# A matrix shift in HBM: the 16 DMA engines' rows spaced 8 apart instead of 4

## The chip, the core and the metric

The kernel runs on one core of a Trainium2 chip. The core has compute engines, which have nothing to do here, and 16 DMA engines, which move data between addresses. SyncE (SP in the profile) issues the transfers; its queue of them is called SPq. One issue is split over the DMA engines, and each contiguous run of it is a packet.

The metric is the time of one execution on the device, in microseconds (us). The kernel before took 813.25 us, the median of three runs from 812.37 to 813.68.

## What is computed

```python
def setup_inputs():
    return {
        "x": np.random.randn(8192, 8192).astype(np.float32),
    }

def reference(x: np.ndarray) -> np.ndarray:
    return np.fft.ifftshift(x)
```

The input is 8192 x 8192 in float32, 268 MB; a row has 32 KB. `ifftshift` of an even size moves everything by half the size in both dimensions, with wrapping: the output's row r is the input's row (r + 4096) mod 8192, and within it the two halves of the columns change places. It is a pure move: 268 MB are read and 268 MB are written.

## The kernel before

There is no on-chip stage: every transfer goes from the input in HBM straight to the output in HBM. The helper `copy` (lines 25 to 29) issues one transfer. Its `dims` are a list of [step, count] pairs, slowest first, in elements; the same list is used on both sides, and only the start differs: on the output's side the row and column given, on the input's side these shifted by half the matrix.

A row is cut into four quarters of 2,048 elements (`piece`), 8 KB each. The outer loop goes over the matrix in blocks of 64 rows (`rows`, 16 engines times `apart` = 4). Within a block four transfers are issued, one for each quarter of the columns, in the order first, third, second, fourth of the output (starts 0, `hc`, `piece`, `hc + piece`, where `hc` is 4,096). Each has 64 rows of 8 KB: 512 KB. In all there are 128 x 4 = 512 issues, all on SP's queue, in program order.

The slowest dimension has 64 entries, and each of the 16 DMA engines gets four neighbouring rows of them, so one engine's rows start 4 rows, 128 KB, after those of the engine before it. Over the four transfers of a block each engine moves its four rows whole. The next block starts 64 rows, 2 MB, further on.

Order and waits are put in by the framework: eight semaphores are used in turn, and SP waits before an issue until an earlier transfer with its semaphore has landed. The profile calls `copy`'s issue line 26.

Of the kernel before, what the change touches and what calls it, by code (L numbers as in the profile page):

```python
# [1 line left out]

# [4 lines left out]


ENGINES = 16  # L10


@with_exitstack
def kernel(
    ctx: ExitStack,
    tc: tile.TileContext,
    x: bass.AP,
    out: bass.AP,
):
    nc = tc.nc  # L20
    R, C = x.shape
    hr = R // 2
    hc = C // 2

    def copy(queue, row, col, dims):
        queue.dma_start(
            out=bass.AP(out.tensor, out.offset + row * C + col, dims),
            in_=bass.AP(x.tensor, x.offset + (row + hr) % R * C + (col + hc) % C, dims),
        )


    apart = 4
    piece = hc // 2
    rows = ENGINES * apart
    for row in range(0, R, rows):
        for col in (0, hc, piece, hc + piece):
            copy(nc.sync, row, col, [[C, rows], [1, piece]])


# [1 line left out]
_INS = ['x']  # L41
_OUTS = [((8192, 8192), 'float32')]


def kernel(**inputs):
    import numpy as _np
    import concourse.bacc as _bacc
    import concourse.tile as _tile
    from concourse import mybir as _mybir
    from concourse.bass_utils import run_bass_kernel_spmd as _run  # L50

    nc = _bacc.Bacc("TRN2", target_bir_lowering=False, num_devices=1)  # L52
    arrays, args = {}, []
    for name in _INS:
        a = _np.ascontiguousarray(inputs[name])
        if a.dtype.kind in "iu":
            a = a.astype(_np.int64)
        arrays[f"in_{name}_dram"] = a
        args.append(nc.dram_tensor(f"in_{name}_dram", a.shape, _mybir.dt.from_np(a.dtype), kind="ExternalInput").ap())
    for i, (shape, dtype) in enumerate(_OUTS):  # L60
        dt = _mybir.dt.from_np(_np.dtype(dtype))
        args.append(nc.dram_tensor(f"out_{i}_dram", shape, dt, kind="ExternalOutput").ap())
    with _tile.TileContext(nc) as tc:
        kernel(tc, *args)
    r = _run(nc, [arrays], core_ids=[0])
    got = tuple(r.results[0][f"out_{i}_dram"] for i in range(len(_OUTS)))
    return got[0]
```

## Time and profile before

| | |
|---|---|
| time, median of 3 runs | 813.25 us |
| lowest to highest | 812.37 to 813.68 us |
| the profiled execution, its own time | 811.93 us |
| its span, first to last instruction | 810.2 us |
| TensorE and the other compute engines | no work; POOL 0.2 us for four constants |
| issues | 512 of 512 KB |
| first issue, last issue | 0.7 us, 797.2 us |

The profile describes one execution. Its page divides the span into 40 equal slices and shows for each the busy share of the DMA engines in tenths and the bytes moved per second, counted once a packet (a copy reads and writes them). Another row gives the packets of each DMA queue and the time they took, as a share of the span of 16 engines. The view of the waits of SP's queue tells how long it stood still and for what. Below the views, the trace has a record of each DMA packet (start, duration, size), without the number of its engine, and one of each increment of a semaphore by a transfer that lands: sixteen for an issue, one an engine.

### The profile page before, as it was taken

Reading aid. Unit: us, or ns where it says so; the run is one execution under the profiler, and the core shown is the slowest. Engines: PE = TensorE matmul, PEld = TensorE weight load, DVE = VectorE, ACT = ScalarE, POOL = GpSimd, SP = SyncE. Lnnn points to the kernel's source line nnn. Section 1 sums busy time; section 2 is a strip of 40 time slices with the busy share of each in tenths; the row PEclk is TensorE's granted clock in tenths of the full one; section 3 lists DMA queues with packets and bytes.
Section 4 is the critical chain, followed back from the end, with each engine's and each line's share of the span. In section 5 each row is a group of like instructions: output and inputs, shape, how many; then the busy total and the mean of one; then the engine's idle time right before and its main releaser. Section 6 shows DMA issues by size and latency. Waiting matters only on the chain. (4 is left out here: it accounts for less than half of the span.)

```text
span 810.2 us, 557 instructions
## 1 busy us (share of the span) xinstructions
POOL 0.2 (0%) x4
## 2 busy tenths in 40 slices
POOL 0000000000000000000000000000000000000000
DMA  8999999999999999999999999999999999999998
GB/s 301 334 328 339 330 335 336 334 329 335 337 336 331 331 335 335 329 335 331 339 333 329 339 336 331 339 330 331 337 336 326 337 330 335 333 328 335 326 328 299
DMA packets 40964, 268.50 MB, mean 331 GB/s; under 512 B 8192, under 2 KB 8192, under 8 KB 8192
## 3 DMA queue, kind: packets, MB, share of 16 engines
q1 hardware_dynamic: 40960, 268.47, 99.1%
q14 instruction: 4, 0.03, 0.0%
HBM read 268.44 MB, written 268.44 MB: 663 GB/s over the span
## 5 line engine op out<-in xcount | busy, mean ns | idle before, releaser
L52 POOL MEMSET const-bfloat16-1.0<- 128x1 bf16 x1 | 0.1, 102 | 0.0
L52 POOL MEMSET const-uint8-127<- 128x1 uint8 x1 | 0.1, 102 | 0.0
L52 POOL MEMSET const-float32-0.0<- 128x1 f32 x1 | 0.1, 99 | 0.2 <-issue 0.2
L52 POOL MEMSET const-float32-1.0<- 128x1 f32 x1 | 0.1, 99 | 0.0
## 6 DMA issues: line engine op xcount, KB each, us to landing
out_dram<-in_x_dram SPq DMA_DIRECT2D x512, 512.0 KB, 12.6
```

Source lines behind the costliest of these rows:

```text
L52: nc = _bacc.Bacc("TRN2", target_bir_lowering=False, num_devices=1)
```

## The change

The 16 engines' groups of rows are 8 rows (256 KB) apart instead of 4, and a block has 128 rows instead of 64. One transfer still gives each engine four neighbouring rows of one quarter of the columns. So a block now takes eight transfers: rows 0 to 3 of each engine's eight in the four quarters, then rows 4 to 7 in the four quarters. The pattern has three dimensions: 16 groups, 4 rows, 2,048 elements.

```diff
-    apart = 4
+    apart = 8
+    part = 4
     piece = hc // 2
-    rows = ENGINES * apart
-    for row in range(0, R, rows):
-        for col in (0, hc, piece, hc + piece):
-            copy(nc.sync, row, col, [[C, rows], [1, piece]])
+    for block in range(0, R, ENGINES * apart):
+        for row in range(block, block + apart, part):
+            for col in (0, hc, piece, hc + piece):
+                copy(nc.sync, row, col, [[apart * C, ENGINES], [C, part], [1, piece]])
```

The number of issues (64 x 2 x 4 = 512), their size, their queue and the size of a packet are as before. The order of the instructions on every engine is the same; only the addresses and the shape of the patterns differ.

## The prediction

> **What bounds the kernel now.** I read the page first: span, the forty slices and the queue rows. Then come the windows view over chosen stretches, the waits of the issuing engine, and the view of all instructions that write the output. Behind these I counted the trace's records of single packets and of landings.
>
> ```profile
> span 810.2 us, 557 instructions
> ...
> DMA  8999999999999999999999999999999999999998
> GB/s 301 334 328 339 330 335 336 334 329 335 337 336 331 331 335 335 329 335 331 339 333 329 339 336 331 339 330 331 337 336 326 337 330 335 333 328 335 326 328 299
> DMA packets 40964, 268.50 MB, mean 331 GB/s; under 512 B 8192, under 2 KB 8192, under 8 KB 8192
> ...
> q1 hardware_dynamic: 40960, 268.47, 99.1%
> ...
> HBM read 268.44 MB, written 268.44 MB: 663 GB/s over the span
> ```
>
> The 16 DMA engines are taken for 99.1% of the span, from the second slice to the last but one, at 326 to 339 GB/s. No compute engine does anything. So the time is the engines' packet time, and the question is what a packet's time is made of. By count the 40,960 packets are 32,768 of 8 KB and 8,192 small ones (16 a transfer, 512 transfers): 2,048 and 512 an engine. The windows view (length, POOL, granted clock, DMA share, GB/s) shows that packets can go faster than they mostly do:
>
> ```profile
> 3.00:5.30 2.30, 0.00 (x0) 1.00 0.94 399
> 5.30:8.00 2.70, 0.00 (x0) 1.00 1.02 370
> 8.00:20.00 12.00, 0.00 (x0) 1.00 0.99 328
> ...
> 100.00:200.00 100.00, 0.00 (x0) 1.00 1.00 334
> ...
> 700.00:797.00 97.00, 0.00 (x0) 1.00 1.00 331
> ```
>
> In the first stretch 399 GB/s; a few us later the rate falls to about 330 and stays there. The packet records say why: of the 114 data packets that start between 2.9 and 5.2 us all took 309 ns. Over the whole span 58% still took 307 to 309 ns, the mean is 390 and one in a hundred takes over 840. A small packet took 9 ns. I read 309 ns as what an engine needs for 8 KB when the memory doesn't hold it up, and the rest as stalls in the memory. For one engine:
>
> - unstalled: 2,048 x 309 ns = 632.8 us, 512 x 9 ns = 4.6 us
> - stalls: 2,048 x (389.9 - 309) ns = 165.6 us
> - sum 803.0 us, which is the 99.1% above. The other 7 us of the 810.2 are 2.1 us before the first packet and 5 of gaps and unequal ends.
>
> **Is the issuing side near a limit?** No:
>
> ```profile
> SPq L26 <- DMA out_dram<-in_x_dram: 525.9, 502, 2.0
> ```
> ```profile
> L26 SPq DMA_DIRECT2D out_dram<-in_x_dram x512: 511/511/695, 0.7 to 797.2; - x171
> ...
> DMA to landing us min/median/max: 4.0/12.6/13.2
> ```
>
> SP's queue needs 511 ns for one issue (512 x 0.511 = 262 us) and stands 526 us waiting for transfers to land. A transfer ends every 810.2 / 512 = 1.58 us and lands 12.6 us after its issue, so some eight (12.6 / 1.58) are always queued.
>
> **The change, part by part.** *Unchanged.* 512 issues of 512 KB, four packets of 8 KB to an engine and issue, the same order of the four quarters, the same bytes: 637.4 us of unstalled time, 0 us of change. Small packets too: 0.
>
> *The issue itself.* Its pattern has three dimensions instead of two (16x4x2048 for 64x2048). The trace shows no such issue. Below: 0, since a cheaper issue gains nothing where SP waits for landings anyway. Above: the longest issue seen, 695 ns, so 184 ns x 512 = 94 us more of SP's queue, all of it inside the 526 us of waiting. I take 0. The cover ends at 1.58 us an issue, three times the usual. No new wait is added, and nothing else stands on that queue before the end.
>
> *The jump between blocks.* Now one issue in four starts a new block, 2 MB on; after it, one in eight steps on by some 4 MB, and one in eight by only 128 KB. What a jump costs is seen in the landing records: the mean time of the 16 landings of an issue moves on by 1.541 us for the second quarter, 1.571 for the third, 1.657 for the fourth and 1.527 for the first of the next block; the mean is 1.573. The step that holds the jump is the cheapest of the four, so a jump as such costs nothing. Bounds: 128 jumps x 46 ns (1.573 - 1.527) = 6 us either way. I take 0.
>
> *The distance between the engines.* This is the part that can move the time, and it moves the 165.6 us of stalls alone. Before, one issue's 64 rows are one run of 2 MB, an engine each 128 KB; after, they lie in 16 clusters of four, an engine each 256 KB, over 4 MB. It matters only if the engines are at the same issue at the same time, and they are: the 16 landings of an issue come within 1.76 us (median; 1.4 to 2.2 for nine issues in ten), about one issue's time. So what the memory sees at once is the 16 engines' rows of one issue or of two neighbours, once for reads and once for writes half the matrix away.
>
> That addresses alone make stalls the trace shows: the four quarters differ only in columns, and they take 1.527 to 1.657 us. With the engines 256 KB apart, their addresses at one moment share one more low bit than with 128 KB, and engines e and e+8 lie 2 MB apart instead of 1 MB. If the memory tells its parts apart by such bits, fewer parts serve the same 16 streams. No row of this trace shows another distance, so I bound it by the quarters. At worst every issue goes like the slowest quarter: 512 x (1.657 - 1.573) = 43 us more. At best every issue goes like the fastest: 512 x (1.573 - 1.527) = 23.6 us less. I take it that one more of the four quarters comes to cost what the slowest does: 128 x 0.084 = 10.8 us. I choose so little because the pattern inside an engine, four rows 32 KB apart in four quarters, stays, and because a part that held up two engines in lockstep would push them out of step, up to the eight queued issues.
>
> On the Trainium skill: DMA: Bandwidth & Descriptors, section Latency and other measured facts, gives copies between HBM tensors whose row pitch is a large power of two, and has them slower the larger it is (207 GB/s at 512 KiB, 164 at 2 MiB, 103 at 4 MiB, 214 when padded). It speaks against this change; if the doubled distance cost what its 512 KiB row lost, the median would be an estimated 813.25 x 214 / 207 = 841. The trace runs at 331 GB/s each way with the engines 128 KB apart, above that page's best, so its figures don't carry over; no run here shows another pitch yet.
>
> **Sum.** 803.0 + 0 + 0 + 0 + 10.8 = 813.8 of packet time, and 7 around it: span 821.0. The profiled execution lay 1.7 us above its span (811.9), and the median shown 1.3 above that, so 813.25 + 10.8 = 824.
>
> **Rivals.** *Wider is better (faster).* With the clusters spread over 4 MB, fewer of the 16 streams meet in the same part of the memory, and the stalls shrink. For it: the stalls are a fifth of the time, 42% of packets have one, and 399 GB/s was once reached. Against it: the distances only grow by one power of two, while the four rows of a cluster, which meet most closely, stay. Its price: half of what separates the mean from the fastest quarter, 512 x 23 ns = 11.8 us, gives 801.5; with all of it, 789.7. It decides as soon as the mean issue takes less than 1.573 us.
>
> *Nothing to tell.* Where data lies in the memory depends on so many address bits that the distance doesn't matter: 813. For it: the stalls look random, each slice within 2% of the mean (326 to 339 of 333 inside). Against: the stalls must stay within 1% (1.66 us) for the time to stay within 0.2%, and the quarters differ by 8%.
>
> *Lockstep bites fully (much slower).* All quarters like the slowest: 856. For it, the narrow landing spread; against, that engines can slip.
>
> *The change doesn't do what it says.* If the three-dimensional pattern is cut up in another way, say on fewer than 16 engines or with an issue over 1.58 us, SP becomes the bound: at 1.62 us an issue 512 x 1.62 = 829 us and 7 around it, 836. Nothing in the trace speaks for it; the outer size, 16, is the number of engines.
>
> **How the numbers follow.** A measurement of this kernel can tell about 0.2%, 1.6 us, from no change: its three runs lie between 812.4 and 813.7. Chances: forecast 0.42 (816 to 840), lockstep in full 0.10, issue bound 0.02: slower 0.54. Wider is better 0.34: faster. Nothing to tell 0.12. The range goes from 795, near the lower bound of 789.7, to 852, near the upper of 856; I leave out 0.07 on each side. The likeliest case's own range is 816 to 840.
>
> **What would show it.** Unstalled packets should stay at 309 ns, and 58% of them or fewer should be so; mean packet some 395 ns instead of 390; GB/s in the middle slices near 329 instead of 333; q1's share still about 99%; issues still 511 ns, with SP's wait for landings longer by the same 11 us; time to landing 12.8 us instead of 12.6. If the issue time is up and the wait gone, the steps on SP are wrong. If the mean packet is under 388 ns, the distance acts the other way, and if it moves while the landings spread far wider than 1.8 us, it is the loss of step and not the addresses of one issue. A q1 share well below 99% would mean idle engines, which no step here has.

## The result

The changed kernel is slower by 0.3%: 815.94 us, the median of ten runs (813.33 to 817.51), against 813.16 us for the kernel before in ten runs (811.43 to 813.68). The ratio is 1.0028, its 95% interval 1.0016 to 1.0041. On another chip, where the kernel before took 824.71 us, it was 1.0034 (1.0020 to 1.0049). So the change costs 2 to 3 us. All further kernels are compared with the kernel before on the same chip, by ratios; there it took 823 to 825 us. A run more than 1.5% above the fastest of its kernel is left out of a ratio, which happened only to two of the four runs with 32 rows apart (1129.7 and 1139.75 us; the other two took 1111.89 and 1114.91).

The page of the changed kernel, the rows that answer to those of before:

```profile
span 815.4 us, 557 instructions
...
DMA  8999999999999999999999999999999999999998
GB/s 301 331 331 331 332 329 331 331 329 328 335 333 333 330 333 327 331 333 331 333 330 325 336 329 333 326 334 334 334 325 332 331 334 330 331 331 334 327 332 295
...
q1 hardware_dynamic: 40960, 268.47, 99.7%
...
HBM read 268.44 MB, written 268.44 MB: 658 GB/s over the span
```

Nothing has changed in kind: the DMA engines are taken from end to end, and the rate is lower by a small amount that is spread over all slices (329 GB/s over the span instead of 331). No slice stands out, so no single place of the program lost the time. The profiled executions exaggerate: this one took 817.17 us, one of the slower of its ten, that of before 811.93, one of the faster; their 5.2 us are twice the difference of the medians.

The windows view (length, POOL, clock, DMA share, GB/s) has the same fast start and the same fall:

```profile
3.00:5.30 2.30, 0.00 (x0) 1.00 1.00 406
5.30:8.00 2.70, 0.00 (x0) 1.00 0.96 364
8.00:20.00 12.00, 0.00 (x0) 1.00 1.01 330
...
100.00:200.00 100.00, 0.00 (x0) 1.00 1.00 330
...
805.00:808.00 3.00, 0.00 (x0) 1.00 1.03 333
```

A share over 1 in a stretch this short says little, since the view counts a packet whole where it starts. The packet records say more. The sum of all packets' time grew by 10.3 us an engine (803.0 to 813.3), the span by only 5.2. Up to 20 packets are under way at once, more than there are engines, so some overlap; but this overlap is nearly the same in both kernels (7.3 and 7.6 us an engine). What shrank is the time in which fewer than 16 are under way: 11.1 us an engine before, 6.3 after. So about half of the added packet time filled gaps and cost nothing.

SP's queue, by the waits and by the view of the output's instructions:

```profile
SPq L26 <- DMA out_dram<-in_x_dram: 500.3, 502, 1.6
```
```profile
L26 SPq DMA_DIRECT2D out_dram<-in_x_dram x512: 571/571/705, 0.7 to 802.2; - x171
...
DMA to landing us min/median/max: 4.1/12.6/13.2
```

An issue with the three-dimensional pattern takes 571 ns, 60 ns more than before. Over 512 issues that is 31 us, and the wait for landings shrank by 26 us. The time went into cover, as far as these rows tell.

By the packet records an unstalled packet still takes 309 ns. More of them are unstalled (61% at 307 to 309 ns instead of 58%), yet the mean is 394.9 ns instead of 389.9: the stalls are fewer and longer (a stalled packet takes 530 ns on average instead of 500).

### The profile page after: what moved, and what is told of

Same layout as the page of the kernel before. It is cut to its first block, busy times and chain, and to the rows that moved or that the text cites. A ratio compares the mean times of both kernels' runs of the same rounds, so it can differ in the third digit from the quotient of the medians.

```text
span 815.4 us, 557 instructions
## 1 busy us (share of the span) xinstructions
POOL 0.2 (0%) x4
## 2 busy tenths in 40 slices
DMA packets 40964, 268.50 MB, mean 329 GB/s; under 512 B 8192, under 2 KB 8192, under 8 KB 8192
## 6 DMA issues: line engine op xcount, KB each, us to landing
out_dram<-in_x_dram SPq DMA_DIRECT2D x512, 512.0 KB, 12.6
```

## The experiments

In the diffs `rows`, `part` and `piece` are as in the code above.

**Is it the pattern's shape, or the issue's 60 ns?** The first kernel keeps the rows and engines of before and takes each engine's rows from the last to the first, so that the pattern has three dimensions.

```diff
 # rev4
-            copy(nc.sync, row, col, [[C, rows], [1, piece]])
+            copy(nc.sync, row + apart - 1, col, [[apart * C, ENGINES], [-C, apart], [1, piece]])
```

> The rows and engines of the kernel before (engines 4 rows apart), but each engine takes its four rows from the last to the first, so that the pattern has three dimensions as in the changed kernel. Theory A (the distance between the engines makes the stalls): issue time about 571 ns as in the changed kernel, yet 813 us, since the distance is the old one. Theory B (the three-dimensional issue costs the 2.8 us): 816. Theory C (the order in which an engine comes back to its own rows, halves of a block and jumps): 813, with the jumps of the kernel before.

Measured: 825.3 against 823.15 us, ratio 1.0027 (1.0014 to 1.0040), issue 571 ns. That is what theory B expected, so the shape comes under suspicion. The next runs are the changed kernel again, two kernels that split it by sides, and one that deals the old rows out one by one:

> The changed kernel once more, beside the kernel before on this chip. If its 0.28% holds from chip to chip, the ratio is 1.002 to 1.004. Theory A (the distance between the engines makes the stalls, convexly: 1.0028 at 8, 1.053 at 16) and theory B (the three-dimensional pattern costs it, as the kernel with descending rows had 1.0027 at the old distance) both expect that.

```diff
 # read8_write4 (read4_write8 is the mirror): k = 0, 1 for the two halves of a block of 128 rows
 # copy(queue, output row, input row, column, output's pattern, input's pattern)
+    four = [[4 * C, ENGINES], [C, part], [1, piece]]
+    eight = [[8 * C, ENGINES], [C, part], [1, piece]]
...
+                copy(nc.sync, block + 64 * k, block + 4 * k, col, four, eight)
```

> Reads with the engines 8 rows apart as in the changed kernel, writes 4 apart as before; the rows within each 128 of the output come out in another order. Theory A: if the stalls come from the reads, 1.003; if from the writes, 1.000. Theory B: 1.003 whichever side. If the two single-sided kernels add up to the whole (one 1.003 and one 1.000, or about 1.0015 each), the distance does it; if both have the whole 1.003, it is the pattern's shape.

> The mirror of the kernel above: reads 4 rows apart as before, writes 8 apart as in the changed kernel; rows within 128 come out in another order. Theory A: 1.003 if the stalls come from the writes, 1.000 if from the reads. Theory B: 1.003.

The output of these two isn't the reference's, as their rows come out in another order; they serve for the time alone.

```diff
 # d1
-            copy(nc.sync, row, col, [[C, rows], [1, piece]])
+            copy(nc.sync, row, col, [[C, ENGINES], [ENGINES * C, part], [1, piece]])
```

> The same 64 rows an issue as before, dealt out one by one: engine e takes rows e, e+16, e+32, e+48, so the engines are one row (32 KB) apart and an engine's own rows 512 KB. The pattern has three dimensions. Theory A in the form of distance between engines: not above 1.000. Theory A in the form of which rows are moved at the same time: 1.000, since they are the same 64. Theory B: 1.003.

Measured: the changed kernel 1.0034 (1.0020 to 1.0049), reads at 8 alone 1.0054 (1.0033 to 1.0074), writes at 8 alone 1.0031 (1.0017 to 1.0044), engines one row apart 1.0006 (0.9991 to 1.0021). The last has the three-dimensional pattern and its 571 ns an issue, and no price that can be measured: the shape alone doesn't cost 0.3%. Each side alone costs about as much as both, or more. Theory B had expected 1.003 of each, so these two speak for the shape, though 1.0054 is more than it expected, and against sides that add up; d1 speaks against the shape. A cleaner comparison on the shape comes below.

**Is it the distance, and if so, how?**

```diff
 # d16, d32, d64: the changed kernel with d = 16, 32 or 64
-    apart = 8
+    apart = d
 # d12, d24 in outline: n = 12 or 24; what is left of each half of the rows with 4 rows apart
+    for half in (0, hr):
+        for block in range(half, half + hr, ENGINES * n):
...
+                    copy(nc.sync, row, col, [[n * C, ENGINES], [C, part], [1, piece]])
```

> The changed kernel with the engines 16 rows (512 KB) apart and four passes over a block. Theory A: more than the changed kernel, 819 or above, because the distance doubles once more. Theory B: 816, the same issue. Theory C: 816 or a little more, as three quarters of the steps to new rows are short ones instead of half.

> Engines 12 rows (384 KB) apart, not a power of two; 504 of the 512 issues so, the last 64 rows of each half with 4 rows apart. Theory A in the form of shared low address bits: 813 or less, since 384 KB leaves the low bit of the distance at 128 KB, as in the kernel before. Theory A in the form of sheer distance: between the changed kernel and 16 apart, 817 to 819. Theory B: 816. Theory C: 816 to 817.

> Engines 24 rows (768 KB) apart, farther than the 16 that cost 5.3%, but not a power of two; 480 of 512 issues so, the rest 4 apart. Theory A1 (sheer distance, or the width of memory that is open at once): above 16 apart, 1.06 or more. Theory A2 (a power of two in the distance: the engines meet in the same part of the memory): near 12 apart, 1.01 to 1.02, since three of the 16 engines' low bits differ as 24 = 16 + 8.

> Engines 64 rows (2 MB) apart, 16 passes over a block of 1,024 rows. Theories A1 and A2: clearly above 16 apart, 1.08 or more. If the cost at 16 is a matter of one particular bit of the address and nothing of the distance, it stays at 1.05 or falls.

> Engines 32 rows (1 MB) apart, the missing point between 16 (1.053) and 64 (1.332). If each doubling takes away half of the places that the engines can be in at once, it lies between, near 1.15; the step from 8 to 16 then is where the price begins to be paid.

Measured, all with clusters of four neighbouring rows:

| engines apart | ratio | 95% interval |
|---|---|---|
| 8 rows (the change) | 1.0028, 1.0034 | 1.0016 to 1.0049 |
| 12 | 1.0115 | 1.0095 to 1.0134 |
| 16 | 1.0531 | 1.0515 to 1.0547 |
| 24 | 1.0034 | 1.0020 to 1.0047 |
| 32 | 1.3512 | 1.3474 to 1.3551 |
| 64 | 1.3324 | 1.3272 to 1.3376 |

Sheer distance falls: 24 apart costs next to nothing beside 16. So does "each doubling takes its share", which expected 1.15 at 32 and more at 64: from 8 to 16 the price is multiplied by about 17, from 16 to 32 by 7, and then it stops. 24 costs the same as 8 (1.0034 on both), and both distances are a multiple of 8 rows but not of 16, which fits the form with shared low bits of the address. 12 doesn't fit it: by that form it is like 4, yet it costs more than 24; that isn't explained here. Rows of the pages of the kernels with 16, with 24 and with 32 rows apart:

```profile
GB/s 282 311 313 312 307 317 312 312 314 315 310 314 309 315 314 316 313 311 316 308 310 316 313 308 313 311 313 314 305 312 311 316 306 313 314 312 319 308 306 274
...
q1 hardware_dynamic: 40960, 268.47, 99.4%
...
out_dram<-in_x_dram SPq DMA_DIRECT2D x512, 512.0 KB, 13.4
```
```profile
HBM read 268.44 MB, written 268.44 MB: 651 GB/s over the span
...
out_dram<-in_x_dram SPq DMA_DIRECT2D x512, 512.0 KB, 12.8
```
```profile
q1 hardware_dynamic: 40960, 268.47, 99.0%
...
HBM read 268.44 MB, written 268.44 MB: 484 GB/s over the span
...
out_dram<-in_x_dram SPq DMA_DIRECT2D x512, 512.0 KB, 17.2
```

The share of the DMA engines is 99% in the fast and in the slow ones: it can't tell a good layout from a bad one. The rate and the time to landing (12.6, 13.4, 17.2 us) can, beside 12.7 to 12.8 us for kernels without a measurable price and with issues of the same size (jump4, seq4, d1). At 32 apart half of the packets still need only 309 ns, but the mean is 534: the rest wait.

**Is it the order of the steps?** In both kernels the landings of the four quarters are uneven, and the forecast took its prices from that.

```diff
 # jump4: even blocks first, then the odd ones
-    for row in range(0, R, rows):
+    for first in (0, rows):
+        for row in range(first, R, 2 * rows):
 # seq4
-        for col in (0, hc, piece, hc + piece):
+        for col in (0, piece, hc, hc + piece):
```

> The transfers of the kernel before, each unchanged, but the blocks of 64 rows in another order: all even ones, then all odd ones, so that every step to new rows is 4 MB instead of 2. Theory C (the jumps and the return to the other half make the 0.3%): 1.002 or more. Theory A (what one issue's 64 rows look like): 1.000.

> The kernel before with the four quarters in the order of the output's columns (0, 1, 2, 3 instead of 0, 2, 1, 3). In both the kernel before and the changed one the fourth quarter's landings come latest after the third's (1.66 and 1.60 to 1.62 us). If the order of the columns makes that, the uneven steps move to another quarter and the time changes by 1% or so, up or down; if it belongs to the step to new rows that follows, it stays: 1.000, with the fourth slow again.

Measured: 1.0001 (0.9991 to 1.0011) and 1.0008 (0.9996 to 1.0021). The length of the jump costs nothing, and neither does the order of the quarters. By the landing records, jump4's issues move on by 1.58, 1.55, 1.59, 1.62, 1.60, 1.56, 1.60 and 1.63 us, about as evenly as the changed kernel's 1.58, 1.57, 1.58, 1.60, 1.59, 1.57, 1.57 and 1.62, and it costs nothing. So the unevenness isn't a price. d1, on one chip with the changed kernel's second run, shows the reverse: its steps are more uneven (means by quarter of 1.54 to 1.67 us against 1.58 to 1.64), and it is the cheaper of the two. Our reading is that a quarter that comes late is followed by one that comes early. In seq4 the fourth quarter's landings are again the latest (1.65 us), but the fourth is the same quarter of the columns in both orders, so this doesn't tell the column from the place in the order.

**Distance of the engines, or the set of rows?** Four kernels with gaps of other kinds, in two pairs. Each pair has one set of 64 rows an issue, dealt out in two ways (the loops around the copies are left out here).

```diff
 # odd8: rows 8e, 8e+2, 8e+4, 8e+6          even2: rows 2e, 2e+32, 2e+64, 2e+96
+    copy(nc.sync, row, col, [[2 * C, 64], [1, piece]])
+    copy(nc.sync, row, col, [[2 * C, 16], [32 * C, 4], [1, piece]])
 # every4_16: rows 16e, 16e+4, 16e+8, ...   every4_4: rows 4e, 4e+64, 4e+128, ...
+    copy(nc.sync, row, col, [[4 * C, 64], [1, piece]])
+    copy(nc.sync, row, col, [[4 * C, 16], [64 * C, 4], [1, piece]])
```

> Engines 8 rows apart, each engine the even rows of its eight in the four quarters, then the odd ones: a two-dimensional pattern (64 rows, two rows apart), so the issue should be back at 511 ns. Theory A: 816 as in the changed kernel or more, since the engines are as far apart and the rows within an engine are spread too. Theory B: 813. Theory C: 816.

> The same 64 rows an issue as in the kernel with even and odd rows (every second row of 128; 1.0106 with the engines 8 apart), dealt out so that the engines are 2 rows apart and an engine's own rows 32. Theory D (the distance between engines decides, since all engines are at the same step of an issue): below 1.003. Theory S (the set of rows that one issue touches decides, whoever moves them): 1.0106 again.

> One issue takes every fourth row of 256; the engines are 16 rows apart as in the kernel with 1.053, but an engine's own rows are 4 apart instead of neighbours. Theory D: about 1.05, as the engines are 16 apart. Theory S: another set of rows, so another price, and the same one as the next kernel.

> The same set of rows as the kernel above, every fourth of 256, dealt out with the engines 4 rows apart as in the kernel before and an engine's own rows 64 apart. Theory D: 1.000 to 1.003. Theory S: as the kernel above.

Measured: every second row, 1.0106 (1.0090 to 1.0122) with engines 8 apart and 1.0128 (1.0104 to 1.0152) with 2. Every fourth row, 1.0080 (1.0064 to 1.0095) with 16 apart and the same 1.0080 with 4. Theory S (the set decides) holds in both pairs within their intervals, and theory D (the distance) in neither; every4_16 has the engines as far apart as the kernel with 1.053. The second pair bears on the shape too. The views of the output's instructions, every4_16 first:

```profile
L26 SPq DMA_DIRECT2D out_dram<-in_x_dram x512: 511/511/681, 0.7 to 815.8; - x171
```
```profile
L26 SPq DMA_DIRECT2D out_dram<-in_x_dram x512: 571/571/729, 0.7 to 815.3; - x171
```

One has two dimensions and 511 ns an issue, the other three and 571; the last issue starts at the same time, and the ratio is the same. So the 60 ns of an issue cost nothing here.

**Large distance without a gap.** The last two, solid8 and solid16, are the kernel before with `apart = 8` and `apart = 16` and nothing else: one issue takes all rows of an engine.

> Engines 8 rows apart as in the changed kernel, but one issue takes all eight rows of each: 128 rows without a gap, 1 MB, 256 issues. Theory S (the set of rows of an issue decides, a run without gaps is best): no more than 1.000, less what 256 x 16 small packets were worth (256 of them an engine at about 6 ns, 1.5 us, 0.2%): 0.998 to 1.000, faster than the changed kernel and possibly than the one before. Theory D (distance): 1.003.

> The same with 16 rows an engine: 256 rows without a gap, 2 MB, 128 issues, engines 16 rows apart as in the kernel with 1.053. At one moment the engines are 16 apart and within one issue's time of each other, so that the rows moved at once are clusters as in that kernel, though the issue as a whole has no gap. Theory S for whole issues: 0.997 to 1.000. Theory S for what is moved within a microsecond or two, or theory D: 1.05.

Measured: 1.0005 (0.9989 to 1.0022) and 0.9994 (0.9975 to 1.0013). Distance 8 and even 16 cost nothing that can be measured if the issue leaves no rows out. The hoped-for gain from fewer small packets didn't show (by the records they take 9 ns each, not the 6 of the expectation). The page of the second, and its view of the output's instructions:

```profile
DMA packets 34817, 268.45 MB, mean 325 GB/s; under 512 B 2048, under 2 KB 2048, under 8 KB 2048
...
q1 hardware_dynamic: 34816, 268.44, 98.7%
...
out_dram<-in_x_dram SPq DMA_DIRECT2D x128, 2048.0 KB, 42.7
```
```profile
L26 SPq DMA_DIRECT2D out_dram<-in_x_dram x128: 596/5948/14699, 0.7 to 781.6; - x128
```

The small packets fell from 8,192 to 2,048, and the mean data packet is 397 ns, against 394 in jump4, another kernel without a measurable price, on another chip. No kernel tried here beats the one before by anything that its interval can tell.

## Why the prediction came out as it did

*What bounds it: right.* Packet time and in it the stalls; 309 ns stayed, in this kernel and in the one that took 35% longer. The forecast looked for 58% of unstalled packets or fewer; they were 61%.

*The issue: right in the time, wrong in the sign to look for.* "Issues still 511 ns" was wrong, they take 571; the 60 ns lie between the bounds of 0 and 184, and the wait for landings covered them, as every4_4 against every4_16 shows. The wait therefore shrank, where the forecast had it grow by 11 us. The time to landing stayed at 12.6 us, where 12.8 was expected.

*The jump: right, 0.* jump4, with jumps twice as long, is at 1.0001.

*The distance between the engines: the term that was mis-sized.* The forecast was "one more of the four quarters comes to cost what the slowest does: 128 x 0.084 = 10.8 us". Measured are 2.8 us here (815.94 - 813.16) and 2.2 on the other chip (826.88 - 824.71), a quarter of it. The direction was right; whether for the forecast's reason isn't shown, since rev4 lost as much at the old distance.

The step that failed has two parts. One is the price list: the quarters' 1.527 to 1.657 us were read as what addresses cost, but jump4 and d1 show that even or uneven steps go with no change in time. The other is the way from packet time to time. The sum kept 7 us around the packets as they were. In the profiled executions the packets' time did grow by 10.3 us, close to the 10.8, and the mean packet came out at the 395 ns foreseen; but what lies around it fell from 7 to 2 us, as gaps were filled. The rest of the miss is in the choice of executions, one of the slower after and one of the faster before (5.2 us of span against 2.8 of medians), so the agreement at 395 ns is in part luck. The profiled executions of the changed kernel and of d1 on the other chip show the same pattern: 6.4 us more packet time in the changed kernel, and a span only 1.6 longer. The list also gave the bounds. They held at 8 apart, but as the worst of any layout 43 us is too little: 16 rows apart cost 43.6 and 32 apart 289. No row of the trace of before could have given the price of a set of rows that it never moves; the honest range was wide on that side.

*The mechanism: partly.* The forecast had engines 256 KB apart meet in fewer parts of the memory at one moment. Powers of two do make large prices (16, 32 and 64 rows apart against 24), and 24 costs what 8 does, so bits of the address that the rows share are the likeliest reading, with 12 against it. But it isn't the distance between engines: the pairs with one set and two distances point to the set of rows, and solid16, whose engines start 16 apart and are within 2.3 us of each other (median spread of an issue's landings), pays nothing. What differs between it and d16 is that d16 keeps to the same four rows of an engine for four issues, some 6 us, while solid16 goes through sixteen. That suggests that the set counts that is worked on for several microseconds, not the one at a moment, but it isn't shown: 2.3 us is the time of some six packets, so the engines of solid16 can stand at six neighbouring rows at one moment, where those of d16 have only four to stand at. No run separates the two. For the large prices the set of rows is thus the best account. For the 0.3% of the change itself the cause stays open: d1 (the old set in the new shape) and solid8 (the new distance without gaps) have no measurable price, which points to the gaps of four rows after every four; but rev4 has no gaps and the old distance and pays 0.27%. Nothing here shows how the memory makes either.

*The rivals.* "Wider is better" fell, as did the lockstep in full (856) and the issue bound (836). "Nothing to tell" was nearest in size: 813, against 815.94. Its reason, that the memory mixes many address bits, is contradicted by 1.35 at 32 apart.

*On the page of the Trainium skill that the forecast weighed* (DMA: Bandwidth & Descriptors, section Latency and other measured facts): its rule that a large power-of-two pitch slows copies agrees with 1.053 at 512 KB and 1.33 to 1.35 at 1 and 2 MB between engines, if one takes the distance between engines for the pitch. The page's first remedy, a few KiB of padding, was not tried; of two distances that are no power of two, 768 KB cost 0.3% and 384 KB 1.2%. As a rule on the distance between engines alone it does not hold here: the same 512 KB cost 0.8% (every4_16) and nothing (solid16). The estimate of 841 worked out from it was too high by 25 us.

*What stays open.* rev4, which has the old set of rows and only takes them in descending order, cost 0.27%, as much as the change; d1 with the same set and no price that shows has an interval that overlaps rev4's from 1.0014 to 1.0021. So the order in an engine may have a part, as large as the whole change. That one side alone with gaps costs as much as both, and that 12 apart costs more than 24, has no explanation here. Which rows an engine takes is read from the pattern; no record has an engine's number. No kernel varies single bits of the address.

## What to carry to other kernels

In a kernel that only moves data, a DMA share of 99% says nothing about how near the limit it is: look at the packets, at the shortest time of one size and at the mean, since the difference is time that packets wait. No layout here won any of it, and the worst made it nearly three times as long (309 ns against means of 390 and 534). Let the rows of an issue form a run without gaps; how they are dealt to the engines and in which order the columns go was then worth 0.3% at most here (rev4), while a gap pattern of a power of two cost up to 35%. And don't price an address pattern by the uneven landings inside one kernel, they even out; measure it, one distance beyond the one you mean, before you believe that a small step is safe.

## What the hardware showed that was not expected

- With clusters of four rows, the price of a power-of-two spacing sets in suddenly: 1.003 at 256 KB, 1.053 at 512 KB, 1.351 at 1 MB, and then no more at 2 MB (1.332).
- The share of unstalled packets doesn't tell the faster kernel: 58% before and 61% after, but also 61 to 62% in jump4 and seq4 and 57% in solid16, which have no measurable price.
- A three-dimensional pattern costs SP's queue 571 ns an issue instead of 511, and an issue of 2 MB with 256 rows a median of 5.9 us (596 ns at best), as if SP's queue were held up while so much is still to be moved (a reading; its waits for landings at that line are none).
- The same kernel took 813 us on one chip and 823 to 825 on five others; the ratio of the change was the same within its interval.
